# One encoder layer on one core: query and key tiles split during the output projections, selection steps set apart, gate tiles loaded in four pieces, gathers spread to near the end

## The chip, the cores and the metric

One core of a Trainium2 chip runs the whole layer as one program. The metric is the device time of one execution in microseconds (us), compared as a median of several runs. Engines: PE (TensorE, matrix products), ACT (ScalarE), DVE (VectorE), POOL (GpSimd, here mainly an issuer of transfers) and SP (SyncE, the issuer of all other transfers). Each engine works its own instructions strictly in the order in which the program emits them.

## The reference, cut to what matters

```python
n = rmsnorm(h, g_mix);  proj = n @ w_in            # h: 16 meta tokens + 512 tokens, D = 1024
y_hy = hyena_branch(...);  y_rg = rglru_branch(...)
merged = sigmoid(gA) * y_hy + sigmoid(gB) * y_rg
h = h + merged @ w_out
h = h + peer(rmsnorm(h, g_ffn), wq, keys, u_tab, v_tab);  out = rmsnorm(h, g_final)[16:]

def peer(x, ...):                                   # 8 heads, 128 keys a half, top 16, 16384 experts
    q = (x @ wq).reshape(B, L, 8, 2, 128)
    s = einsum('blhpd,hpkd->blhpk', q, keys);  ts, ti = top_k(s, 16)
    cand = ts[..., 0, :, None] + ts[..., 1, None, :];  cs, ci = top_k(cand, 16)
    experts = e1 * 128 + e2;  g = softmax(cs)       # e1, e2: ti taken at ci // 16, ci % 16
    act = gelu(x . u_tab[experts]) * g
    return sum over experts of act * v_tab[experts]
```

## The kernel before, in words

Every product is made exact to about float32 by splitting each operand into a float16 high and a low part (`split`, L80: ACT writes the high part, L81; DVE the low part, L82) and running three float16 matmuls (`mm3`, L84). Weights come as a list of jobs, [128, 1024] float32 tiles of 512 KB. `w_load` (L94) issues a job's load on SP into one of three buffers `wf` (six once the pool `gp` exists), `w_prep` (L103) splits it into one of four buffers `wh`, and `w_get(i)` (L120) first prepares up to job i + 2. So the split of a weight is emitted two jobs ahead of its matmuls.

The order of the work: the **front** (Hyena and RG-LRU branches); the **output projections**, eight pairs of jobs hy_out and rg_out merged into `mg`, then eight jobs w_out, a sum of squares and the second norm; the **Q stage**, 16 query projections with 16 weights wq and 2 key tiles (jobs w0 to w0 + 17), scores, and the first top-16 selections; then the **expert stage**. It computes, for 384 of the 512 tokens, all 128 blocks of experts densely: step u_e is gelu(x . u) of block e (24 matmuls of 384 columns), step v_e adds block e's weighted values (18 matmuls of 512 columns). The job list `seq` runs u_0 to u_100, then v_96, u_101 ... alternating until u_127, then v_0 to v_95. The results of u_0 to u_95 are spilled to DRAM (`sd`) and loaded again (`sin`). The last 128 tokens (tile tt = 3) take gathered rows instead: 128 gathers of u rows and 128 of v rows (`gather`, L1093, an indirect transfer of 128 rows of 4 KB from POOL's queue, four row buffers), each followed by one DVE instruction (L1128, L1149).

Beside u_0 to about u_93 the program places **selection and routing**: 64 top-16 selections (`top16`), then `routing`: `select(tt)` for each token tile (eight candidate top-16s, index arithmetic, a softmax whose tanh runs on ACT, transposes on PE, expansion copies on ACT) and `tokens(tt)`, which in 16 blocks of 8 tokens builds one-hot products `oh` and `og` on DVE. `flush` multiplies those of two blocks earlier on PE into `ps_gt` (three buffers), and ACT moves them to `stg`, from where they go to DRAM as the gate table `gd`. `both` interleaves tokens(0) with select(1), and tokens(1) with select(2).

How much of it stands beside one step is set by hand. Each `yield` of these generators names its cost on DVE and ACT in microseconds, and `pull` (L800) takes from the generators until a step's budget is used up; what was overdrawn is carried on. A `yield 0` ends the step. The budgets are 3.2 in a query step and `PACE` = 3.7 in a u step, where each gather step taken is also charged 1.3. `gathers(rate)` allows `rate` gather steps per step: `GRATE` = 0.7 beside routing, 1.35 after it, and from v_0 on (268 - steps done) / (E0 - 12). When routing has ended, or at u_93 at the latest, the remaining routing is forced out, the pools change, and the first gate tile `gin` (16 experts, 3 MB) is loaded: eight experts at once and eight one step later. Later gate tiles are loaded whole, at the fifth step of every 16 (`gload`, `pmul`).

Of the kernel before, what the change touches and what calls it, by code (L numbers as in the profile page):

```python
# [66 lines left out]
class Kernel:  # L67
    def __init__(self, ctx, tc, a, out):
        self.ctx, self.tc, self.nc, self.a, self.out = ctx, tc, tc.nc, a, out
        self.keep = ctx.enter_context(tc.tile_pool(name="keep", bufs=1))  # L70
        self.wp = ctx.enter_context(tc.tile_pool(name="wp", bufs=1))
        self.jobs = []
        self.loaded = {}
        self.ready = {}
        self.nl = 0
        self.evac = None
        self.nr = 0
        self.gp = None

    def split(self, hi, lo, src, s):  # L80
# [13 lines left out]
    def w_load(self, upto):  # L94
        while self.nl <= min(upto, len(self.jobs) - 1):
            src, s, n, dst = self.jobs[self.nl]
            p = self.wp if self.gp is None or self.nl % 2 else self.gp
            t = p.tile([128, D], F32, name="wf", bufs=self.WF)
            self.nc.sync.dma_start(t[:, :n], src)  # L99
            self.loaded[self.nl] = t  # L100
            self.nl += 1

    def w_prep(self, upto):  # L103
        while self.nr <= min(upto, len(self.jobs) - 1):
            i = self.nr
            self.w_load(i)
            src, s, n, dst = self.jobs[i]
            t = self.loaded.pop(i)
            if dst is None:
                h = self.wp.tile([128, 2, D], F16, name="wh", bufs=self.WH)  # L110
                hi, lo = h[:, 0, :n], h[:, 1, :n]
                self.ready[i] = h
            else:
                hi, lo = dst()
                self.ready[i] = None
            self.split(hi, lo, t[:, :n], s)
            self.nr += 1
            self.w_load(i + self.WF * (1 if self.gp is None else 2))
# [165 lines left out]
    def front(self, xt, acc):  # L284
# [220 lines left out]

        mp = ctx.enter_context(tc.tile_pool(name="mp", bufs=1, side="right"))
        mg = fr.tile([128, 2, 8, SEQ], F16, name="mg", tag="n")
        for i in range(8):
# [15 lines left out]
            nc.vector.scalar_tensor_tensor(ma, ma, (S_W * S_YR) / (S_HO * S_YH), mb, op0=OP.mult, op1=OP.add)  # L524
            self.split(mg[:, 0, i, :], mg[:, 1, i, :], ma, 0.5 * S_M / (S_W * S_YR))
        sq, qs = {}, None
        for i in range(8):
# [12 lines left out]
            if i == 0:  # L540
                qs = sq.pop(0)
        pn = psum.tile([128, 2, 512], F32, name="ps_n2", tag="pg")
        for k, t in enumerate((qs, sq[6], sq[7])):
# [271 lines left out]
    def peer(self, acc):  # L815
# [40 lines left out]
        def half_topk(h, t):  # L856
            for pr in range(2):
                for tt in (3, 0, 1, 2):
                    hp = 2 * h + pr
                    self.top16(qp, t[:, pr, tt, :], tv[:, tt, hp, :], ti[:, tt, hp, :], 128)  # L860
                    yield 1.3

# [3 lines left out]
        for i in range(16):  # L866
            if i == 0:
                ws = [self.w_get(w0 + k) for k in range(2)]
                pj = {k: psum.tile([128, 512], F32, name="ps_q", tag="s", bufs=3) for k in range(2)}
# [12 lines left out]
            if i == 3:  # L882
                self.w_prep(w0 + 6)
            if i % 2 == 1 and i >= 3:
# [4 lines left out]
            if i >= 3:  # L889
                self.pull(3.2, 3.2)  # L890

# [19 lines left out]

        def gload(k, parts=((0, EB),)):
            if k < 128 // EB:
                b = order[EB * k] // EB
                if b not in gin:
                    gin[b] = vp.tile([128, NCH, EB, CH], F32, name="gin", bufs=2)
                for i, n in parts:
                    o = CH * (EB * b + i)
                    nc.sync.dma_start(gin[b][:, :, i:i + n, :].rearrange("p c e t -> p c (e t)"),
                                      gd[:, :, o:o + CH * n].rearrange("c p n -> p c n"))  # L920

# [6 lines left out]
        def pmul(i):  # L928
            if i >= 128:
                return  # L930
            e = order[i]
            if i % EB == 4:
                gload(i // EB + 1)
            sload(i + 6)
# [56 lines left out]
        for pos, (kind, e) in enumerate(seq):  # L991
            if kind == "u":
# [14 lines left out]
                if vp is None and (route not in self.bgq or e == E0 - 3):  # L1007
# [10 lines left out]
                    ob += [ups.tile([128, 2, 512], F32, name="ob%d" % k, tag="ob%d" % k) for k in range(3)]  # L1018
                    gload(0, ((0, 8),))
                    e0 = e  # L1020
                elif vp is not None and e == e0 + 1:
                    gload(0, ((8, EB - 8),))
                    nc.vector.tensor_scalar(self.ident, self.ident, S_P * S_V, None, op0=OP.mult)
                continue
# [9 lines left out]
            if i >= 128 - E0:  # L1034
                if rate is None:
                    rate = (268 - self.gsteps) / (E0 - 12.0)
                gathers(rate)
            else:
                gathers(self.GRATE[1])
# [41 lines left out]
    LV = 5  # L1081
    PACE = (3.7, 3.7)
    TB = 8
    GRATE = (0.7, 1.35)
    LAG = 2
# [13 lines left out]
    def gather_setup(self, psum, e12, w):  # L1099
# [9 lines left out]
        nc.vector.tensor_tensor(xg, x2[:, 0, :, TD:], x2[:, 1, :, TD:], OP.add)  # L1109
        yield 2.0  # L1110
        for b in range(2):
            pt = psum.tile([128, 512], F32, name="ps_xn", tag="t", bufs=2)
# [63 lines left out]
    def routing(self, p, psum, tv, ti, iota, iof, gd):  # L1176
        nc = self.nc
        eT = {}

        def select(tt):  # L1180
            t4 = p.tile([128, 256, 4], F16, name="t4")
# [53 lines left out]
            sh = [128, 8, TOPK]  # L1235
            nc.vector.tensor_tensor(t, cv, cv[:, :, 0:1].to_broadcast(sh), OP.subtract)
            nc.scalar.activation(t, t, AF.Tanh, scale=-0.5)
            yield 0.3
            yield 0
            nc.vector.tensor_scalar(w, t, -1.0, 1.0, op0=OP.mult, op1=OP.add)  # L1240
# [6 lines left out]
            yield 2.4  # L1247
            yield 0
            if tt == 3:
# [4 lines left out]
            nc.tensor.transpose(pt[:, 128:256], e12[:, 0, :], self.ident)  # L1254
            nc.tensor.transpose(pt[:, 256:384], w.rearrange("p h k -> p (h k)"), self.ident)

            ed = p.tile([128, 128, 2, 4], F16, name="ed", bufs=2)
# [4 lines left out]
            wt = pt[:, 256:384, None].to_broadcast([128, 128, 4])  # L1262
            nc.scalar.activation(gd4[:, :, 0, :], wt, AF.Copy, scale=S_G)
            nc.vector.scalar_tensor_tensor(gd4[:, :, 1, :], wt, S_G, gd4[:, :, 0, :], op0=OP.mult, op1=OP.subtract)
            eT[tt] = ed, gd4
            yield 1.0, 2.0

# [194 lines left out]
```

## Time and profile before

| | us |
|---|---|
| runs shown (three) | 1713.04, 1717.74, 1720.14; median 1717.74 |
| the profiled execution | 1716.81 (span from first to last instruction 1715.0) |
| PE busy | 1619.6 (94% of the span) |
| DVE busy | 1402.8 (82%) |
| ACT busy | 767.4 (45%) |
| POOL busy | 368.9 (22%) |
| mean granted clock of PE | 0.982 of full |

The span is what the trace covers; the 1.8 us outside it belong to launch and end. Busy time of DVE counts the overlap of consecutive instructions once in the page's totals; in sums by mean duration the overlap is counted twice, so the prediction uses distances from start to start where it can. In tables by stage the columns are busy time (and count) of each engine, PE's granted clock (1.00 is 2.4 GHz, 0.50 is 1.2 GHz), the busy share of the 16 DMA engines and what they moved.

### The profile page before, as it was taken

Reading aid. Unit: us, or ns where it says so; the run is one execution under the profiler, and the core shown is the slowest. Engines: PE = TensorE matmul, PEld = TensorE weight load, DVE = VectorE, ACT = ScalarE, POOL = GpSimd, SP = SyncE. Lnnn points to the kernel's source line nnn. Section 1 sums busy time; section 2 is a strip of 40 time slices with the busy share of each in tenths; the row PEclk is TensorE's granted clock in tenths of the full one; section 3 lists DMA queues with packets and bytes.
Section 4 is the critical chain, followed back from the end, with each engine's and each line's share of the span. In section 5 each row is a group of like instructions: output and inputs, shape, how many; then the busy total and the mean of one; then the engine's idle time right before and its main releaser. Section 6 shows DMA issues by size and latency. Waiting matters only on the chain. (4 is left out here: it accounts for less than half of the span.)

```text
span 1715.0 us, 25010 instructions
## 1 busy us (share of the span) xinstructions
PE 1619.6 (94%) x9451; PEld 905.7 (53%) x9451; DVE 1402.8 (82%) x2422; ACT 767.4 (45%) x1055; POOL 368.9 (22%) x321
## 2 busy tenths in 40 slices
PE   7999999899989987998998998899999999999998
PEld 5675666444435544665665665455554444444443
DVE  7736679985478998998997996788889889999984
ACT  5433379962243333443754764343333333324342
POOL 0000000000000001222221223344445444445500
PEclk9999999999999999999998999999999999999999
DMA  5332142223323347678887899999999999999981
GB/s 194 124 121 74 40 146 65 71 80 106 113 86 96 89 146 249 236 239 306 280 312 263 299 343 348 350 383 314 366 359 361 406 395 393 400 395 407 395 307 50
DMA packets 134970, 416.19 MB, mean 243 GB/s; under 512 B 12064, under 2 KB 39968, under 8 KB 131392
## 3 DMA queue, kind: packets, MB, share of 16 engines
q1 hardware_dynamic: 97776, 279.72, 46.0%
q0 software_dynamic: 37072, 134.86, 21.0%
q8 instruction: 74, 1.21, 0.3%
q14 instruction: 48, 0.39, 0.1%
HBM read 368.39 MB, written 46.14 MB: 242 GB/s over the span
## 5 line engine op out<-in xcount | busy, mean ns | idle before, releaser
L981 PE MATMUL ob<-wh,pt 128*128 128x512 f16 x2304 | 511.9, 380 | 19.2 <-DVE wh L82 11.8
L82 DVE SCALAR_TENSOR_TENSOR wh<-wf,wh 128x1024 f16<-128x1024 f32 (+1 forms) x340 | 409.2, 1207 | 103.5 <-ACT wh L81 102.5
L81 ACT ACTIVATE wh<-wf 128x1024 f16<-128x1024 f32 (+1 forms) x340 | 352.5, 1041 | 142.1 <-DMA wf<-in_peer_v 48.3
L981 PEld LDWEIGHTS <-pt 128*128 128x128 f16 x2304 | 225.9, 98 | 288.6 <-issue 23.0
L88 PE MATMUL ps_e<-x,wh 128*128 128x384 f16 x1024 | 337.1, 329 | 16.2 <-DVE wh L82 16.2
L86 PE MATMUL ps_e<-x,wh 128*128 128x384 f16 x1024 | 337.6, 330 | 1.9 <-ACT gs L955 1.9
L87 PE MATMUL ps_e<-x,wh 128*128 128x384 f16 x1024 | 337.5, 330 | 0.0
L1095 POOL DMA_INDIRECT rows<-in_peer_un,gidx x128 | 182.1, 1423 | 446.8 <-DVE junk L1128 394.0
L88 PEld LDWEIGHTS <-wh 128*128 128x128 f16 x1504 | 148.3, 99 | 149.1 <-DVE wh L82 23.6
L1095 POOL DMA_INDIRECT rows<-in_peer_v,gidx x128 | 180.1, 1407 | 187.3 <-DVE acc L1149 154.9
L87 PEld LDWEIGHTS <-wh 128*128 128x128 f16 x1504 | 148.3, 99 | 129.5 <-issue 12.1
L86 PEld LDWEIGHTS <-wh 128*128 128x128 f16 x1504 | 148.6, 99 | 120.9 <-issue 4.7
L1149 DVE SCALAR_TENSOR_TENSOR acc<-rows,dots,acc 128x1024 f32<-128x1024 f32 x127 | 162.9, 1282 | 20.6 <-DMA rows<-in_peer_v,gidx 19.8
L943 ACT ACTIVATE pt<-pf 128x384 f16<-128x384 f32 x128 | 66.6, 520 | 226.2 <-DVE pf L936 167.5
L1128 DVE SCALAR_TENSOR_TENSOR junk<-rows,xn 128x1024 f32<-128x1024 f32 x128 | 156.2, 1220 | 5.6 <-DMA rows<-in_peer_un,gidx 5.0
L271 PE MATMUL ps_p<-n,wh 128*128 128x264 f16 x960 | 111.9, 277 | 2.0 <-DVE wh L82 2.0
L955 ACT ACTIVATE gs<-ps_e 128x384 f32<-128x384 f32 x96 | 47.2, 491 | 132.3 <-PE ps_e L88 121.0
L271 PEld LDWEIGHTS <-wh 128*128 128x128 f16 x960 | 94.2, 98 | 20.5 <-issue 3.5
L1290 ACT ACTIVATE stg<-ps_gt 128x512 f32<-128x512 f32 x96 | 93.1, 1083 | 15.8 <-PE ps_gt L1283 10.5
L947 DVE TENSOR_TENSOR pt<-pf,pt 128x384 f16<-128x384 f32 x128 | 70.9, 554 | 12.4 <-ACT pt L943 12.4
L86 PE MATMUL ps_p<-n,wh 128*128 128x512 f16 x192 | 73.3, 382 | 0.1
L87 PE MATMUL ps_p<-n,wh 128*128 128x512 f16 x192 | 73.3, 382 | 0.0
(276 smaller groups left out, 1832.7 us busy)
## 6 DMA issues: line engine op xcount, KB each, us to landing
wf<-in_peer_u SPq DMA_DIRECT2D x128, 512.0 KB
wf<-in_peer_v SPq DMA_DIRECT2D x128, 512.0 KB
gd<-stg SPq DMA_DIRECT2D x24, 1024.0 KB
wf<-in_w_in SPq DMA_DIRECT2D x44, 512.0 KB
gin<-gd SPq DMA_DIRECT2D x7, 3072.0 KB
sd<-gs SPq DMA_DIRECT2D x48, 384.0 KB
sin<-sd SPq DMA_DIRECT2D x48, 384.0 KB
wf<-in_wq SPq DMA_DIRECT2D x16, 512.0 KB
```

Source lines behind the costliest of these rows:

```text
L81: self.nc.scalar.activation(hi, src, AF.Copy, scale=s)
L82: self.nc.vector.scalar_tensor_tensor(lo, src, s, hi, op0=OP.mult, op1=OP.subtract)
L86: mm(ps, lh, rh, start=first, stop=False)
L87: mm(ps, lh, rl, start=False, stop=False)
L88: mm(ps, ll, rh, start=False, stop=last)
L271: nc.tensor.matmul(ps[:, h, :HL], x, n[:, y, c, h * HL:(h + 1) * HL], start=(c == 0 and x is lh and y == 0), stop=(c == 7 and x is ll))
L947: nc.vector.tensor_tensor(pt[i][:, 1, :], pf.pop(i), pt[i][:, 0, :], OP.subtract)
L981: mm(ob[tt][:, h, :], pp[:, x, sl], w[:, y, h * 512:(h + 1) * 512], start=first and k == 0, stop=last and k == 2)
L1095: self.nc.gpsimd.indirect_dma_start(out=r, out_offset=None, in_=table, in_offset=bass.IndirectOffsetOnAxis(ap=self.gidx[:, j:j + 1], axis=0))
L1128: nc.vector.scalar_tensor_tensor(junk, rows.pop(0), 1.0, self.xn, op0=OP.mult, op1=OP.mult, accum_out=self.dots[:, j:j + 1])
L1149: nc.vector.scalar_tensor_tensor(acc2, r, d, acc2, op0=OP.mult, op1=OP.add)
L1290: nc.scalar.activation(st[c][:, :, o:o + 4].rearrange("p e t -> p t e"), ps, AF.Copy, scale=S_P / S_G)
```

## The change

1. While the output projections run, 18 jobs (16 wq, 2 key tiles) are loaded through POOL's queue, split, and written back to DRAM as float16 pairs (`pre`), 1.75 per pair of projections and then 1.5 per w_out job. In the Q stage SP loads these pairs straight into `wf` or `wh` buffers, and the keys into their tile, with no split.
2. Pacing: a key top-16 is charged 1.65 instead of 1.3; the query budget is 4.4 and 4.2 instead of 3.2, `PACE` 4.2, `GRATE` 0.8 and 1.5.
3. In `select` and `gather_setup`, steps that hand over between engines are set apart by further yields. For tiles 0 and 3 each is a `yield 0`; for tiles 1 and 2, which run interleaved with `tokens`, one or two yields of 0.001.
4. The gate tile is loaded in four pieces of six token chunks each: the first one at four successive steps from the end of routing, later ones at steps 3, 5, 7 and 9 of 16.
5. The final gather rate spreads the rest over E0 - 5 steps instead of E0 - 12.

```diff
+    NPRE = 18
+    PS = (1.75, 1.5)
+    def pre_load(self):
+        while self.npl < min(self.np + 4, self.NPRE):
+            t = self.pool_p.tile([128, D], F32, name="pw", bufs=5)
+            self.nc.gpsimd.dma_start(t, self.jobs[self.w0 + self.npl][0])
...
+    def presplit(self, k, load=True):
+        self.pcr += k
+        while self.pcr >= 1.0:
+            self.pcr -= 1.0
...
+            h = self.pool_p.tile([128, 2, D], F16, name="ph", bufs=5)
+            self.split(h[:, 0, :], h[:, 1, :], self.pl.pop(self.np), self.jobs[self.w0 + self.np][1])
+            self.nc.gpsimd.dma_start(self.pre[self.np], h)
+            self.np += 1
+            if load:
+                self.pre_load()
@@ w_load
+            if self.is_pre(self.nl):
...
+                    nm, nb = ("wf", self.WF) if k % 2 else ("wh", self.WH)
+                    t = self.wp.tile([128, 2, D], F16, name=nm + "p", tag=nm, bufs=nb)
+                    self.nc.sync.dma_start(t, self.pre[k])
@@ front
+        self.pool_p = mp
+        self.pre_load()
...
+            self.presplit(self.PS[0])
...
+            self.presplit(self.PS[1] if i < 7 else 0)
...
@@ peer
-                    yield 1.3
+                    yield 1.65
-                self.pull(3.2, 3.2)
+                self.pull(4.4, 4.2)
-        def gload(k, parts=((0, EB),)):
+        def gload(k, q):
...
+                cs = slice(q * NCH // 4, (q + 1) * NCH // 4)
+                nc.sync.dma_start(gin[b][:, cs].rearrange("p c e t -> p c (e t)"),
+                                  gd[cs, :, CH * EB * b:CH * EB * (b + 1)].rearrange("c p n -> p c n"))
-            if i % EB == 4:
-                gload(i // EB + 1)
+            if i % EB in (3, 5, 7, 9):
+                gload(i // EB + 1, (i % EB - 3) // 2)
-                    rate = (268 - self.gsteps) / (E0 - 12.0)
+                    rate = (268 - self.gsteps) / (E0 - 5.0)
-    PACE = (3.7, 3.7)
+    PACE = (4.2, 4.2)
-    GRATE = (0.7, 1.35)
+    GRATE = (0.8, 1.5)
@@ routing, select
+        def gap(tt, n):
+            if tt in (0, 3):
+                yield 0
+            else:
+                for _ in range(n):
+                    yield 1e-3
             nc.vector.tensor_tensor(t, cv, cv[:, :, 0:1].to_broadcast(sh), OP.subtract)
+            yield 0.3
+            yield from gap(tt, 2)
             nc.scalar.activation(t, t, AF.Tanh, scale=-0.5)
-            yield 0.3
-            yield 0
+            yield 0.0, 0.3
+            yield from gap(tt, 2)
...
             nc.tensor.transpose(pt[:, 256:384], w.rearrange("p h k -> p (h k)"), self.ident)
+            yield from gap(tt, 1)
...
             nc.scalar.activation(gd4[:, :, 0, :], wt, AF.Copy, scale=S_G)
+            yield 0.0, 2.0
+            yield from gap(tt, 2)
             nc.vector.scalar_tensor_tensor(gd4[:, :, 1, :], wt, S_G, gd4[:, :, 0, :], op0=OP.mult, op1=OP.subtract)
```

## Rows read from the trace of the kernel before

**Rows 1.** The page's first part: the span, and PE's busy time with its number of instructions.

```profile
span 1715.0 us, 25010 instructions
PE 1619.6 (94%) x9451; PEld 905.7 (53%) x9451; DVE 1402.8 (82%) x2422; ACT 767.4 (45%) x1055; POOL 368.9 (22%) x321
```

**Rows 2.** Busy time by stage: the front; the output projections; the Q stage; u_0 to u_22; u_23 to u_92; u_93 to the first matmuls of v_96; the alternation of u and v; v_0 to v_79. Columns: stretch, its length, busy time and count of PE, PEld, DVE, ACT and POOL, granted clock, DMA share, GB/s.

```profile
0.00:374.40 374.40, 354.48 (x2197) 228.10 (x2198) 278.83 (x402) 221.69 (x316) 6.11 (x64) 0.98 0.30 101
374.40:479.30 104.90, 99.43 (x453) 44.77 (x453) 59.62 (x76) 32.31 (x44) 0.00 (x0) 0.99 0.34 108
479.30:575.70 96.40, 94.47 (x553) 47.27 (x553) 80.24 (x287) 37.33 (x53) 0.00 (x0) 0.98 0.29 93
575.70:691.60 115.90, 96.37 (x587) 56.16 (x584) 106.25 (x427) 40.03 (x57) 5.49 (x5) 0.97 0.56 180
691.60:1028.40 336.80, 320.71 (x2395) 207.75 (x2393) 305.31 (x497) 183.85 (x242) 79.88 (x48) 0.97 0.80 284
1028.40:1088.80 60.40, 48.46 (x303) 28.17 (x301) 36.07 (x51) 24.67 (x33) 17.71 (x13) 0.89 0.97 344
1088.80:1310.60 221.80, 221.80 (x1183) 115.64 (x1182) 188.76 (x268) 83.07 (x115) 98.55 (x77) 1.00 0.97 355
1310.60:1643.50 332.90, 319.78 (x1490) 147.93 (x1489) 305.18 (x351) 117.41 (x158) 161.16 (x114) 1.00 1.03 398
```

**Rows 3.** What PE waited for, over the whole span: who, for whom, us in total, times, longest.

```profile
PE ps_gt L1283 <- ACT stg L1290: 18.4, 12, 5.8
PE ps_e L88 <- DVE wh L82: 16.2, 13, 2.2
PE ob L981 <- DVE wh L82: 11.8, 16, 1.5
...
PE ob L981 <- ACT pt L943: 6.1, 1, 6.1
...
PE ps_xn L1114 <- DVE xg L1109: 4.6, 1, 4.6
...
PE ps_q L88 <- DVE wh L82: 1.7, 1, 1.7
```

**Rows 4.** The same table as in rows 2 for short stretches: u_5 and u_6; u_21 to u_29; u_45 and u_46; u_70 and u_71; u_93 and u_94; u_101 and v_96.

```profile
596.20:607.10 10.90, 8.14 (x50) 4.53 (x48) 10.49 (x51) 2.91 (x5) 0.00 (x0) 1.00 0.49 132
683.80:718.90 35.10, 35.10 (x218) 21.16 (x217) 32.24 (x90) 14.41 (x21) 6.95 (x4) 1.00 0.68 243
782.20:800.00 17.80, 10.80 (x67) 6.39 (x65) 16.77 (x25) 4.81 (x7) 4.28 (x3) 0.81 0.84 304
906.50:921.80 15.30, 11.48 (x66) 6.80 (x64) 13.28 (x21) 4.76 (x7) 5.02 (x3) 0.78 0.69 251
1028.40:1048.70 20.30, 14.48 (x116) 9.37 (x114) 12.90 (x16) 11.25 (x13) 5.15 (x3) 0.83 0.98 373
1072.10:1088.80 16.70, 10.58 (x45) 4.71 (x43) 8.76 (x15) 5.68 (x9) 2.81 (x2) 0.80 0.85 338
```

**Rows 5.** DVE in order of time (start, duration, instruction): a key top-16 from its first MAX8 to the next one's, and one stretch with the one-hot products, a gather's product and the low part of a weight.

```profile
505.46 0.29 DVE L1170 MAX8 tv<-sc 128x8 f32<-128x128 f32 x1
...
506.91 0.28 DVE L1170 MAX8 tv<-sc 128x8 f32<-128x128 f32 x1
...
1028.62 1.23 DVE L1305 TENSOR_TENSOR oh<-iota,ed 128x2048 f16<-128x2048 f16 x1
1029.76 1.22 DVE L1128 SCALAR_TENSOR_TENSOR junk<-rows,xn 128x1024 f32<-128x1024 f32 x1
...
1030.90 1.22 DVE L82 SCALAR_TENSOR_TENSOR wh<-wf,wh 128x1024 f16<-128x1024 f32 x1
1032.04 1.22 DVE L1309 TENSOR_TENSOR og<-oh,gd 128x2048 f16<-128x2048 f16 x1
```

**Rows 6.** What DVE waited for in the output projections, 374.4 to 479.3 (columns as in rows 3).

```profile
DVE ma L522 <- PE ps_hy L88: 14.7, 7, 2.4
...
DVE xt L536 <- PE ps_o L88: 8.5, 8, 1.6
```

**Rows 7.** What ACT waited for in selection, routing and the start of the values, 575.7 to 1088.8 (columns as in rows 3).

```profile
ACT wh L81 <- DMA wf<-in_peer_u: 34.7, 8, 8.8
ACT sm_t L1237 <- DVE sm_t L1236: 29.6, 4, 9.8
ACT ed L1260 <- PE ps_r L1255: 11.2, 3, 3.7
```

**Rows 8.** The page's part on transfers: tiles, issuing queue, count, size of one.

```profile
wf<-in_peer_u SPq DMA_DIRECT2D x128, 512.0 KB
...
gin<-gd SPq DMA_DIRECT2D x7, 3072.0 KB
...
sin<-sd SPq DMA_DIRECT2D x48, 384.0 KB
```

**Rows 9.** POOL's gather instructions from u_23 to u_92 (busy time, mean ns of one, idle time before them and for whom).

```profile
L1095 POOL DMA_INDIRECT rows<-in_peer_un,gidx x48 | 79.9, 1664 | 266.7 <-DVE junk L1128 266.7
```

**Rows 10.** The same in the alternation of u and v.

```profile
L1095 POOL DMA_INDIRECT rows<-in_peer_un,gidx x63 | 79.6, 1263 | 101.1 <-DVE junk L1128 94.0 <-issue 5.2 <-DVE wh L82 0.9
```

**Rows 11.** The chain that ended last, two pieces of it (start, us, what).

```profile
1056.99 20.66 DMA wf<-in_peer_u
...
1350.72 9.38 DMA rows<-in_peer_v,gidx
```

More of the change, by code (lines that the diff above doesn't have):

```diff
@@ L78, in __init__, with pre_drain, is_pre @@
         self.gp = None
+        self.dr0 = ctx.enter_context(tc.tile_pool(name="dr0", bufs=1, space=DRAM))
+        self.pre = self.dr0.tile([self.NPRE, 128, 2, D], F16, name="pre")
+        self.pool_p = None
+        self.np = self.npl = 0
+        self.pcr = 0.0
+        self.pl = {}
+        self.w0 = None
+    NPRE = 18
[4 more added lines that the diff above has]
+            self.nc.gpsimd.dma_start(t, self.jobs[self.w0 + self.npl][0])
+            self.pl[self.npl] = t
+            self.npl += 1
+    def presplit(self, k, load=True):
+        self.pcr += k
+        while self.pcr >= 1.0:
+            self.pcr -= 1.0
+            if self.np >= self.NPRE or (not load and self.np >= self.npl):
+                return
+            h = self.pool_p.tile([128, 2, D], F16, name="ph", bufs=5)
[4 more added lines that the diff above has]
+                self.pre_load()
+    def pre_drain(self):
+        self.pcr = 0.0
+        self.presplit(self.npl - self.np, False)
+    def is_pre(self, i):
+        return self.w0 is not None and self.w0 <= i < self.w0 + self.NPRE
     def split(self, hi, lo, src, s):
@@ L96, in w_load @@
             src, s, n, dst = self.jobs[self.nl]
+            if self.is_pre(self.nl):
+                k = self.nl - self.w0
+                assert k < self.np
+                if dst is None:
+                    nm, nb = ("wf", self.WF) if k % 2 else ("wh", self.WH)
+                    t = self.wp.tile([128, 2, D], F16, name=nm + "p", tag=nm, bufs=nb)
+                    self.nc.sync.dma_start(t, self.pre[k])
+                    self.loaded[self.nl] = t
+                else:
+                    self.loaded[self.nl] = dst
+                self.nl += 1
+                continue
             p = self.wp if self.gp is None or self.nl % 2 else self.gp
@@ L108, in w_prep @@
             t = self.loaded.pop(i)
+            if self.is_pre(i):
+                self.ready[i] = None
+                if dst is None:
+                    self.ready[i] = t
+                else:
+                    for r, x in enumerate(dst()):
+                        self.nc.sync.dma_start(x, self.pre[i - self.w0, :, r, :])
+                self.nr += 1
+                self.w_load(i + self.WF)
+                continue
             if dst is None:
@@ L541, in front @@
                 qs = sq.pop(0)
+            self.presplit(self.PS[1] if i < 7 else 0)
+        self.pre_drain()
+        assert self.np == self.NPRE, self.np
         pn = psum.tile([128, 2, 512], F32, name="ps_n2", tag="pg")
@@ L868, in peer @@
                 ws = [self.w_get(w0 + k) for k in range(2)]
+                self.w_prep(w0 + 6)
                 pj = {k: psum.tile([128, 512], F32, name="ps_q", tag="s", bufs=3) for k in range(2)}
@@ L881, in peer @@
                              x2[:, 0, c, :], x2[:, 1, c, :], c == 0, c == 7)
-            if i == 3:
-                self.w_prep(w0 + 6)
             if i % 2 == 1 and i >= 3:
@@ L916, in gload @@
                     gin[b] = vp.tile([128, NCH, EB, CH], F32, name="gin", bufs=2)
[L917 to L920, printed above, removed]
+                cs = slice(q * NCH // 4, (q + 1) * NCH // 4)
+                nc.sync.dma_start(gin[b][:, cs].rearrange("p c e t -> p c (e t)"),
+                                  gd[cs, :, CH * EB * b:CH * EB * (b + 1)].rearrange("c p n -> p c n"))
         def sload(i):
@@ L1018, in peer @@
                     ob += [ups.tile([128, 2, 512], F32, name="ob%d" % k, tag="ob%d" % k) for k in range(3)]
-                    gload(0, ((0, 8),))
+                    gload(0, 0)
                     e0 = e
-                elif vp is not None and e == e0 + 1:
-                    gload(0, ((8, EB - 8),))
-                    nc.vector.tensor_scalar(self.ident, self.ident, S_P * S_V, None, op0=OP.mult)
+                elif vp is not None and e in (e0 + 1, e0 + 2, e0 + 3):
+                    gload(0, e - e0)
+                    if e == e0 + 1:
+                        nc.vector.tensor_scalar(self.ident, self.ident, S_P * S_V, None, op0=OP.mult)
                 continue
@@ L1178, in routing @@
         eT = {}
+        def gap(tt, n):
+            if tt in (0, 3):
+                yield 0
+            else:
+                for _ in range(n):
+                    yield 1e-3
         def select(tt):
@@ L1247, in select @@
             yield 2.4
-            yield 0
+            yield from gap(tt, 2)
             if tt == 3:
@@ L1263, in select @@
             nc.scalar.activation(gd4[:, :, 0, :], wt, AF.Copy, scale=S_G)
+            yield 0.0, 2.0
+            yield from gap(tt, 2)
             nc.vector.scalar_tensor_tensor(gd4[:, :, 1, :], wt, S_G, gd4[:, :, 0, :], op0=OP.mult, op1=OP.subtract)
             eT[tt] = ed, gd4
-            yield 1.0, 2.0
+            yield 0.7
         pend = []
```

## The prediction, made before the changed kernel was run

> **What bounds the kernel now.** The first view is the busy time of the engines: PE is busy for 94% of 1715.0 us [rows 1], so a gain can only come from the 95 us in which PE stands, and from stretches in which its clock is down. The second view is busy time by stage [rows 2]. A stage's loss is its length less PE's busy time, plus (1 - granted clock) times its length. That gives 23.0 us for u_0 to u_22 (19.5 idle and 3.5 by the clock), 26.2 for u_23 to u_92 (16.1 and 10.1), 18.5 from u_93 to v_96 (11.9 and 6.6), nothing in the alternation of u and v, and 13.1 from v_0 to v_79. The front loses more, but the change does not touch it.
>
> The third view, PE's waits, tells why [rows 3]: 16.2 us for low parts of weights from DVE beside the u steps, 18.4 for a free `ps_gt`, which ACT empties, 4.6 for `xg` before the transposes, 6.1 before v_96, 11.8 for low parts in the v steps. The fourth view is steps [rows 4]. Nine undisturbed u steps take 35.1 us, 3.90 each; with that, the alternation (26 u and 31 v steps in 221.8 us, rows 2) gives 3.88 for a v step. u_5 and u_6 take 10.9 us, 5.45 each. The cause is on DVE: a key top-16 takes 1.45 us from start to start and a weight's low part 1.14 [rows 5], and three selections and one low part are 5.49. DVE sets the pace there, and PE waits.
>
> The waits for `ps_gt` have another cause. ACT waited 29.6 us in four places for the difference that the softmax's tanh reads, and 11.2 in three for the transposes [rows 7]. Behind these in ACT's order stand the copies that free `ps_gt`. At two such places PE lost 7.0 and 3.8 us idle, with a mean clock of 0.81 and 0.78 [rows 4].
>
> **The change part by part.** All sums are made against the profiled execution, 1716.8 us, 1.8 outside its span; the median of the runs is 0.9 above it.
>
> *Splits moved to the output projections.* 18 low parts of 1.14 us, 20.5 us of DVE, and as many high parts on ACT leave the Q stage for a stage in which DVE is busy for 59.6 of 104.9 us and ACT for 32.3 [rows 2]. A pair of projections lasts (24 + 12) products, 7.8 us by the same rate as the v step's (3.88 for 18). DVE stands about 2.1 us of it before the sums, 14.7 over 7 [rows 6], and 1.75 splits are 2.0 us. It fits. Transfers are 18 loads, 18 stores and 18 loads again instead of 18 loads, 19 MB more; the DMA share is 0.34 there. What could show is the first load, issued when the branch buffers come free, as ACT stands before the first split until it has landed; two jobs of lead cover most. I take a cost of 1.5 us, bounds 0 and, by rival D, much more.
>
> One row speaks against the place of issue. POOL's gathers take 1664 ns beside the one-hot products and 1263 later [rows 9, 10], so its issuing does depend on what DVE does. The Trainium skill, page SBUF — State Buffer, section SBUF: two separate sides, says that a transfer issued by GpSimd has its descriptors written by that engine, which an exclusive lock of DVE's on their shared port can hold up. Here it would be 0.4 us on each of 36 issues, which nobody waits for with four loads ahead.
>
> *What the Q stage does with it.* It gets 4.4 for selections charged 1.65, by the rule of `pull` 35 selections before u_0, where it had 33. Most of the DVE time that comes free idles. The wait of 1.7 us [rows 3] goes.
>
> *u_0 to u_22.* 4.2 / 1.65 is 2.55 selections a step: 2.55 x 1.45 + 1.14 = 4.83, still 0.93 above 3.90. Some ten steps wait so, less the 1.3 us of score products at u_8: 8.0. The index work of tiles 3 and 0 behind them is charged about 1.12 times its length (1.25 against 1.14 for a one-hot product), so 4.2 is 3.75, with the low part 4.89, 0.99 too much over four full steps: 4.0. Together 12. The wait for `xg` goes, as a step now lies between it and the transposes, and with it the fall of the clock, which came in that wait. 23.0 becomes 12: gain 11; bounds 0 (the DVE waits grow by what the others give) and 15.
>
> *u_23 to the end of routing.* I counted what `pull` takes by the yields. Routing ends beside u_89 (before: u_93, by force). From u_23 to u_88 DVE has 317 us by the distances of rows 5 and the lines of the selection, and PE 298 (66 steps of 3.90, 90 groups of four gate products at 0.45, an estimate from busy 320.7 less 10.1 less 70 steps in rows 2). DVE is 19 us longer; it starts some 6 ahead, so 13 are waits. Before, DVE had 310 and PE 313, and the loss was ACT's. Now the tanh comes two token steps after the difference (2 x 1.14 us of DVE work or more), the copies two after the transposes; ACT is busy only 184 of 337 us and catches up. I leave 3 us of these waits. 26.2 becomes 16: gain 10; bounds 0 and 20.
>
> *The end of routing.* Eight copies and six product groups remain in one step, before it was ten and eight, with DVE now up to 5 us behind PE. The loss was 9.3, 5.8 idle and 3.5 by the clock [rows 4]; I take 9: gain 0.5, bounds -4 and 4.
>
> *The first v step.* 9.4 us are lost at u_101 and v_96 [rows 4]: a load of `wf` took 20.66 us [rows 11] behind 3 MB of gate tile [rows 8], asked for nine steps before v_96. The tile is now asked for in four pieces from u_89 on, 13 steps ahead. The same bytes pass in a busy stage (0.97), so I keep 2: gain 7.5, bounds 0 and 9.4.
>
> *The alternation.* 1.5 gathers a step instead of 1.35: two weights, three rows of 0.52 MB each and 0.2 MB of gate tile in 7.78 us, 362 GB/s. The next stage moves 398 [rows 2], so it holds; a cost of 1, bounds 0 and 6.
>
> *The values.* By the counts 139 gather steps are done at v_0 before, 158 after. The rate falls from (268 - 139) / 84 = 1.54 to (268 - 158) / 91 = 1.21. A v step moves a weight (0.52 MB), the gathers, 0.2 of `gin` and 0.2 of `sin`: 1.72 MB before, which at 398 GB/s [rows 2] is 4.3 us; now 1.55, 3.90 against PE's 3.88. DVE, busy 305 of 332.9 us, loses 0.33 x 1.2 = 0.4 us a step. So the waits of 13.1 us nearly go; smaller pieces also spare `sin` and `wf` the queue behind 3 MB. Left: 2 us, gain 11; bounds 4 and 13. The last gather now ends beside about v_88, and its closing sums fit before v_95.
>
> Sum: 1.7 + 11 + 10 + 0.5 + 7.5 + 11 - 1.5 - 1 = 39.2. 1716.8 - 39 = 1678 us, clock included.
>
> **The rivals.**
>
> B, DVE stays the bound: what ACT's waits gave up, DVE's lag takes, since `PACE` asks 4.89 us of DVE against 3.90 of PE wherever no gate products stand. For it: 33 selections become only 35, and DVE exceeds PE by 19 us in routing. Against: DVE stood idle in ACT's waits before. Without the 11 and 10: 1716.8 - 18 = 1699.
>
> C, transfers bind the expert stage. The trace moves 398 GB/s over 332.9 us [rows 2] and 344 with a share of 0.97 around v_96. If the gathers at 1.5 with the pieces of the gate tile let u_90 to v_96 lag, the gain of 7.5 goes, and a V stage at 380 GB/s (4.08 a step) waits 0.2 x 88 = 18 us. Then 1678 + 7.5 + 18 = 1704. The sum above needs none of the next sentences. The Trainium skill, page DMA: Bandwidth & Descriptors, section Specifications, gives about 358 GB/s as what HBM gives one core. By that a v step took 4.33, and the time would be 1678 + 7.5 + 0.45 x 88 = 1725. The trace's 398 speaks against it.
>
> D, on the other side: the splits' loads are late. ACT stands before each of the 18 until its tile has landed, the high parts of the projections' weights stand behind it, and PE stops. 18 splits lie in eight pairs and three steps, 8 x 7.8 + 3 x 5.2 = 78 us, 4.3 us each. POOL's queue has to pass a load and a store in that time, and a store waits for its split. One transfer takes 8 to 9 us from issue to landing by the chain [rows 11]. With four loads ahead it holds. If only one load were under way at a time, a period were 8 us, 66 us more: 1678 + 66 = 1744. The change turns into a loss from 4.3 + 39 / 18 = 6.5 us a period on.
>
> **How the numbers follow.** Chances: forecast 0.65, B 0.19, C 0.10, D 0.06. A measurement of this kernel can tell 0.5%, 8.6 us, from no change. The bounds of no change are 1708 and 1725. The forecast, B and most of C lie below; of B I put 0.03 and of C 0.02 into no change, and of C 0.02 beside D into slower. Faster 0.87, same 0.05, slower 0.08. With every term halfway to its better bound the sum is 51 (1666), halfway to its worse one 17 (1700); the forecast's own range, 1662 to 1695, lies about there. The range of 8 in 10 takes in B and most of C and, below, routing's upper bound: 1658 to 1707.
>
> **What would show it.** Right: no wait for `ps_gt` over 3 us before routing's end, none for `xg`; no fall of the clock between u_19 and u_88; waits for low parts beside u_5 to u_80 of 20 to 28 us in total; v_96 within 3 us of u_101's end; v_0 to v_79 in about 320 us; no wait over 1 us in the output projections. Wrong: waits of ACT for `pw` (rival D), long waits of PE for low parts in routing above 30 us (B), or a V stage that keeps 4.1 us a step (C).

## The result, and the profile after

The changed kernel took 1677.2 us (median; 1676.4 to 1679.1) where the kernel before took 1715.4 beside it on the same chip: ratio 0.9775, 95% interval 0.9751 to 0.9798. Forecast were 1678, with a range of 1658 to 1707. The profiled execution took 1676.4, 1.8 outside its span.

The page's first part, to hold against [rows 1]:

```profile
span 1674.6 us, 25103 instructions
PE 1611.2 (96%) x9451; PEld 901.4 (54%) x9451; DVE 1405.8 (84%) x2422; ACT 768.1 (46%) x1055; POOL 362.9 (22%) x357
```

DVE and ACT do what they did before, to 3 us; POOL has 36 instructions more, the transfers of the early splits. So no engine was given less work: the 40 us are waits and clock.

Busy time by stage, with the columns of [rows 2]: the front; the output projections; the Q stage; u_0 to u_22; u_23 to u_88; u_89 to the first matmuls of v_96; the alternation; v_0 to v_79.

```profile
0.00:375.30 375.30, 355.80 (x2197) 229.01 (x2198) 278.86 (x401) 221.58 (x316) 6.14 (x64) 0.98 0.30 100
375.30:483.30 108.00, 100.41 (x454) 44.38 (x454) 76.84 (x93) 48.13 (x60) 19.09 (x36) 0.99 0.82 299
483.30:578.30 95.00, 94.86 (x553) 47.50 (x553) 64.60 (x291) 22.11 (x37) 0.00 (x0) 0.97 0.21 68
578.30:683.40 105.10, 94.10 (x588) 55.05 (x586) 98.43 (x375) 39.35 (x56) 6.22 (x5) 1.00 0.61 188
683.40:996.60 313.20, 303.53 (x2316) 196.07 (x2314) 309.39 (x531) 181.23 (x238) 85.33 (x51) 0.99 0.87 305
996.60:1059.10 62.50, 56.15 (x364) 33.83 (x362) 41.34 (x57) 24.73 (x33) 24.49 (x20) 0.97 1.03 401
1059.10:1287.00 227.90, 226.18 (x1200) 117.37 (x1201) 203.62 (x275) 87.61 (x121) 99.45 (x88) 1.00 1.00 374
1287.00:1603.10 316.10, 316.10 (x1489) 148.13 (x1488) 292.60 (x339) 117.73 (x160) 122.14 (x96) 1.00 1.03 395
```

Three lines matter. The projections became longer (104.9 to 108.0). The Q stage has DVE busy for 65 of 95 us: the room that the early splits made is not used. And v_0 to v_79 has PE busy for its whole length, 316.1 for 332.9. The sixth and seventh lines can't be set beside those of [rows 2] as they stand: there the cut (1088.8) lies at the end of v_96, here at its start. From the start of v_96 to v_0 the alternation took 228.3 before and 227.9 after.

What PE waited for, over the whole span, against [rows 3]:

```profile
PE ps_e L126 <- DVE wh L120: 16.3, 16, 1.7
...
PE ps_gt L1362 <- ACT stg L1369: 3.8, 11, 0.8
PE ps_e L124 <- ACT gs L1019: 2.3, 1, 2.3
PE ob L1045 <- ACT pt L1007: 2.1, 1, 2.1
PE ob L1045 <- DVE wh L120: 1.7, 2, 1.4
PE ps_hy L126 <- DVE wh L120: 1.6, 2, 0.9
```

`ps_gt` fell from 18.4 to 3.8, the low parts of the v steps from 11.8 to 1.7, `xg` is gone; the low parts of the u steps stayed (16.2 and 16.3): a step still asks more time of DVE than of PE. ACT, in selection and routing, with [rows 7] to compare:

```profile
ACT sm_t L1313 <- DVE sm_t L1310: 13.3, 4, 5.5
...
ACT ed L1337 <- PE ps_r L1331: 3.5, 2, 2.8
```

29.6 became 13.3, with the longest at 5.5 instead of 9.8; the wait for the transposes fell from 11.2 to 3.5.

### The profile page after: what moved, and what is told of

Same layout as the page of the kernel before. It is cut to its first block, busy times and chain, and to the rows that moved or that the text cites. A ratio compares the mean times of both kernels' runs of the same rounds, so it can differ in the third digit from the quotient of the medians.

```text
span 1674.6 us, 25103 instructions
## 1 busy us (share of the span) xinstructions
PE 1611.2 (96%) x9451; PEld 901.4 (54%) x9451; DVE 1405.8 (84%) x2422; ACT 768.1 (46%) x1055; POOL 362.9 (22%) x357
## 3 DMA queue, kind: packets, MB, share of 16 engines
q0 software_dynamic: 42256, 153.73, 24.4%
## 4 chain that ended last, share of the span: by engine, by line
PE 55%; issue 18%; DVE 12%; POOL 6%; DMA 5%; ACT 4%; POOLq 0%; DVEq 0%; SPq 0%; ACTq 0%
PE ob L1045 29%; POOL rows L1160 6%; PE ps_p L331 4%; DVE wh L120 2%; PE ps_e L126 2%; PE ps_e L124 2%; PE ps_e L125 2%; DMA rows<-in_peer_un,gidx 2%; PE ps_q L125 2%; PE ps_q L126 1%; PE ps_q L124 1%; DMA wf<-in_peer_u 1%; PE ps_p L124 1%; PE ps_p L125 1%; PE ps_p L126 1%
## 5 line engine op out<-in xcount | busy, mean ns | idle before, releaser
L1045 PE MATMUL ob<-wh,pt 128*128 128x512 f16 x2304 | 506.4, 379 | 3.9 <-ACT pt L1007 2.1
L120 DVE SCALAR_TENSOR_TENSOR wh<-wf,wh 128x1024 f16<-128x1024 f32 (+1 forms) x324 | 388.0, 1207 | 74.2 <-ACT wh L119 73.9
L119 ACT ACTIVATE wh<-wf 128x1024 f16<-128x1024 f32 (+1 forms) x324 | 335.9, 1039 | 94.3 <-DMA wf<-in_peer_u 37.6
L126 PE MATMUL ps_e<-x,wh 128*128 128x384 f16 x1024 | 335.5, 328 | 16.3 <-DVE wh L120 16.3
L126 PEld LDWEIGHTS <-wh 128*128 128x128 f16 x1376 | 135.0, 98 | 137.2 <-DVE wh L120 29.6
L1160 POOL DMA_INDIRECT rows<-in_peer_v,gidx x128 | 156.5, 1223 | 239.6 <-DVE acc L1215 219.9
L125 PEld LDWEIGHTS <-wh 128*128 128x128 f16 x1376 | 135.2, 98 | 109.9 <-issue 6.3
L124 PEld LDWEIGHTS <-wh 128*128 128x128 f16 x1376 | 135.1, 98 | 103.9 <-issue 1.7
L331 PEld LDWEIGHTS <-wh 128*128 128x128 f16 x960 | 94.4, 98 | 20.4 <-issue 3.5
L1011 DVE TENSOR_TENSOR pt<-pf,pt 128x384 f16<-128x384 f32 x128 | 71.4, 558 | 12.7 <-ACT pt L1007 11.8
## 6 DMA issues: line engine op xcount, KB each, us to landing
sin<-sd SPq DMA_DIRECT2D x48, 384.0 KB, 13.1
```

The costliest lines, as they stand in the source:

```text
L119: self.nc.scalar.activation(hi, src, AF.Copy, scale=s)
L120: self.nc.vector.scalar_tensor_tensor(lo, src, s, hi, op0=OP.mult, op1=OP.subtract)
L124: mm(ps, lh, rh, start=first, stop=False)
L125: mm(ps, lh, rl, start=False, stop=False)
L126: mm(ps, ll, rh, start=False, stop=last)
L331: nc.tensor.matmul(ps[:, h, :HL], x, n[:, y, c, h * HL:(h + 1) * HL], start=(c == 0 and x is lh and y == 0), stop=(c == 7 and x is ll))
```

## The experiments

Each kernel was timed against the kernel before on its own chip, so they are compared by ratio; an interval is some 0.2 to 0.3% either way, 3 to 5 us. Where less counts, the traces are compared step by step.

**Part 3 undone** (selection steps together again).

```diff
-            yield 0.3
-            yield from gap(tt, 2)
             nc.scalar.activation(t, t, AF.Tanh, scale=-0.5)
-            yield 0.0, 0.3
-            yield from gap(tt, 2)
+            yield 0.3
+            yield 0
...
```

> The changed kernel with part 3 undone: the selection steps stand together again, as in the kernel before; all else as changed. Theory (the routing stage gained because ACT no longer stands before a difference or a transpose with the copies that free ps_gt behind it): the waits of PE for ps_gt and xg and the falls of the clock come back. Before they were 18.4 and 4.6 us and the clock cost 10.1 us in u_23 to u_92; with the budgets of the changed kernel I expect 20 to 35 us more than the changed kernel's 1677, so about 1702, with 15 us or more of waits for ps_gt and at least four new falls of the clock. Rival (the DVE time freed and the new budgets ended the waits): within 5 us of 1677, and waits for ps_gt under 6 us.

Measured: 1710.9, ratio 0.9956 (0.9939 to 0.9972), some 31 us above the changed kernel's. Two groups of PE's waits, and one of ACT's, came back:

```profile
PE ps_gt L1356 <- ACT stg L1363: 24.4, 12, 8.5
...
PE ps_xn L1179 <- DVE xg L1174: 4.6, 1, 4.6
```

```profile
ACT sm_t L1310 <- DVE sm_t L1309: 38.9, 4, 11.8
```

and the granted clock (0.96) in u_23 to u_84:

```profile
689.40:1007.80 318.40, 292.00 (x2204) 188.81 (x2203) 295.90 (x485) 171.83 (x226) 80.55 (x49) 0.96 0.81 280
```

All of it came back, and more than there had been before (24.4 us of waits for `ps_gt` against 18.4). That the larger budgets let DVE fall further behind at such a place would explain the rest; no run tests it. By the steps of the two traces, 32.5 us apart in span, 6.4 lie in u_0 to u_22 and 22.5 in routing. The other 4 come after routing: 9.8 us are lost beside u_93 and u_94 (one wait of 7.5 for `gs`), where the changed kernel loses 5.8 from u_99 on; that these belong to the order is not shown. The theory holds, for some 29 us.

**Part 3 alone**, on the kernel before (the same lines, added).

> The kernel before with part 3 alone: the selection steps set apart, nothing else changed. Theory (part 3 carries the gain of selection and routing by itself): the 18.4 us of waits for ps_gt fall below 8, the 4.6 for xg go, and most of the falls of the clock; DVE's own lag takes some of it back, and more of routing is forced at u_93. The running sum gives 24 us less; 1717 less 24 is 1693, taken between 1688 and 1700; the value stage keeps its 13 us of waits. Rival (it needs the room that the other parts make): 10 us or less, 1707 or more.

Measured: 1695.0, ratio 0.9871 (0.9842 to 0.9900), 22 us less. PE's waits for `ps_gt` fell from 18.4:

```profile
PE ps_gt L1296 <- ACT stg L1303: 7.8, 8, 2.2
```

The value stage keeps its loss and adds to it (v_0 to v_79 in 337 us for 333). One part makes more than half of the whole gain, alone as well as last.

**Part 1 undone** (`NPRE` = 0; job w0 + 6 prepared at the fourth query step again, as before).

> The changed kernel with part 1 undone: the 18 query and key tiles are split in the Q stage again, with its larger budget of 4.4; all else as changed. Theory (the freed DVE time of the Q stage mostly idles, and PACE alone sets the waits of u_0 to u_22): the output projections come back by about 3 us (108.0 to 105), the Q stage loses 2 to 5 (DVE then has some 85 of 95 us of work there, waits for low parts return), u_0 to u_22 lose 0 to 3 as DVE starts them later; in sum 1677 with 4 either way. Rival (the freed time is what u_0 to u_22 gained 10.8 us from): about 1688, with 10 us or more lost there.

Measured: 1673.7, ratio 0.9744 (0.9728 to 0.9761): the changed kernel is not slower without its early splits but faster, by 5 us by ratio, where the intervals just overlap, and by 3.4 by its trace. The output projections:

```profile
376.20:481.10 104.90, 99.43 (x453) 44.74 (x453) 59.62 (x76) 32.32 (x44) 0.00 (x0) 0.99 0.33 108
```

are as before, the Q stage takes 96.8 for 95.0, and u_0 to u_22 take 105.0, in the changed kernel 105.1. So no part of the gain of u_0 to u_22 came from freed DVE time. These stages make 1.3 of the 3.4 us (3.1 less 1.8); 2.2 lie in the alternation, which here has no wait.

**Part 2 undone** (1.3, 3.2 and `PACE` 3.7; gather rates kept).

> The changed kernel with the budgets of before: 1.3 for a selection, 3.2 in a query step, PACE 3.7; the gather rates 0.8 and 1.5 stay. 33 selections before u_0; 3.7 / 1.3 is 2.85 selections a step, 4.13 us and 1.14 for the low part, 5.27 of DVE; routing is not done at u_93 and its rest is forced there. Theory: u_0 to u_22 give back 6 of the 10.8 us they gained (xg stays cured), and the forced end costs 4 to 10 more; 1687 to 1693, taken 1688. Rival (the budgets don't matter beside the steps set apart): 1677 to 1680.

Measured: 1680.4, ratio 0.9785 (0.9768 to 0.9803): the rival's figure was right, 2 us by ratio, less than the noise. But not because budgets don't matter. By the steps of the trace, u_0 to u_22 lose 3.9 us more. From u_23 to u_84 it takes 277 us for 294: 24 groups of gate products fewer stand there (10.7 us at the 0.445 a group used below), and 6.7 us less is lost. The rest of routing is forced into u_93, which alone takes 27.4, with 22 groups in it; 8.2 us more are lost from there to u_98. Gains and losses cancel but for the 3.0 us between the spans.

**A larger query budget alone.**

```diff
-                self.pull(4.4, 4.2)
+                self.pull(5.8, 5.8)
```

> The changed kernel with a larger query budget: 5.8 in place of 4.4, so 46 selections stand before u_0 where it has 35; PACE stays 4.2. DVE idles some 30 of the 95 us of the Q stage in the changed kernel, and 11 selections of 1.45 us are 16. Theory (the u steps wait because PACE asks 4.89 us of DVE in a step in which PE has 3.90, and that is so as long as selection and routing last): the waits stay and only routing ends earlier, by five steps; no gain, 1674 to 1679. Rival (the waits are the sum of the DVE work that is left): 9 to 11 us faster, 1667.

Measured: 1678.8, ratio 0.9776 (0.9758 to 0.9793), no gain. Routing ended at u_84, five steps earlier, and there the kernel stood at 975.3 us; the changed one, less five steps of 3.90, at 977.1. The waits for low parts stayed (16.3 before, 14.5 here), as the theory said; what was won went later, in the longer of the two waits for `gs`, beside u_91:

```profile
PE ps_e L126 <- DVE wh L120: 14.5, 16, 1.6
PE ps_e L124 <- ACT gs L1019: 11.0, 2, 8.7
```

**The larger query budget with a smaller `PACE`** (6.2 and 3.8).

> The changed kernel with a query budget of 6.2 (49 selections before u_0) and PACE 3.8 in place of 4.2. Theory: with 3.8, 3.8 / 1.65 is 2.3 selections a step, 3.3 us, and 1.14 for the low part, 4.5 of DVE; routing lasts to u_93 as its work starts seven steps earlier. A running sum of the three engines in the order of the program, from the durations of the rows, gives 9.6 us of waits of PE up to u_101 where it gives 24.9 for the changed kernel (measured there some 25), so 15 us less, 1662; some 3 may go at the start, as DVE has 80 us of work in the 77 from the first selection to u_0. Rival (waits for low parts come late because their loads or ACT are late, not by DVE's pace): no change, 1677.

Measured: 1665.3, ratio 0.9697 (0.9679 to 0.9714), 13 us less. From u_23 to u_84 it takes 278 us for 294; ten groups of gate products fewer stand there (4.5 us), the other 11.5 are loss that is gone. The waits of PE:

```profile
PE ps_e L126 <- DVE wh L120: 9.4, 7, 2.5
...
PE ob L1045 <- ACT pt L1007: 6.0, 1, 6.0
```

The first is nearly halved. The second, at v_96, is back: routing now ends eight steps ahead of it instead of twelve. It takes the gathers too, for with fewer of them and the same end of routing it is gone (both edits, below). A smaller `PACE` alone was not run, so how the 13 us divide between the two edits is not shown.

**Part 4 undone** (gate tiles whole, the first in two halves).

> The changed kernel with part 4 undone: the first gate tile in two halves, later ones whole; all else as changed. Theory (the pieces help the first v step only): u_99 to v_96 lose 9 to 10 us in place of about 5.7, and 0 to 3 us of waits come at the later gate tiles; 1679 to 1684, taken 1681. Rival (3 MB transfers in front of weights and spilled values made the waits of the value stage): 11 us or more of waits come back from v_0 to v_79, 1690 or more.

Measured: 1679.9, ratio 0.9774 (0.9758 to 0.9791), the same as changed. The trace shows 3.8 us more from u_85 to v_96, with a wait of 3.6 before u_98, and v_0 to v_79 to 0.1 us as in the changed kernel: the pieces do nothing for the value stage.

**The old gather rates.**

```diff
-                    rate = (268 - self.gsteps) / (E0 - 5.0)
+                    rate = (268 - self.gsteps) / (E0 - 12.0)
-    GRATE = (0.8, 1.5)
+    GRATE = (0.7, 1.35)
```

> The changed kernel with the gather rates of before: 0.7 and 1.35 a step, the rest spread over E0 - 12 steps; all else as changed. By the count of yields 141 gather steps are then done at v_0 and the rate is 1.51 a v step, where the changed kernel has 158 and 1.21. Theory (the value stage was held up by its gather rate): 9 to 13 us of waits for low parts come back from v_0 to v_79, the alternation and the first v step give back 0 to 2; about 1687. Rival (the smaller pieces of the gate tile cured the value stage): at most 3 us, so 1677 to 1680.

Measured: 1690.8, ratio 0.9834 (0.9817 to 0.9850), 10 us above the changed kernel by ratio, 16 by the spans, all of it from v_20 to v_79. Is it DVE or the bytes? The old rates ask more of both, so DVE's part was halved: the sum takes half of the columns of each gathered row, the same rows are moved, and the values of the other half are left out.

```diff
-                nc.vector.scalar_tensor_tensor(acc2, r, d, acc2, op0=OP.mult, op1=OP.add)
+                nc.vector.scalar_tensor_tensor(acc2[:, :512], r[:, :512], d, acc2[:, :512],
+                                               op0=OP.mult, op1=OP.add)
```

> The kernel with the old gather rates once more, with each sum of a gathered v row taken over only half of its columns: DVE's instruction is half as long, and the transfers are the same (the values of the last 128 tokens are left out in the other half). From v_0 to v_79 the run with the old rates took 328.4 us, the changed kernel 312.2. Theory (the old rate asks 1.72 MB in a step of 3.93 us, 437 GB/s, where both move some 400: bytes bind): the waits stay, v_0 to v_79 take 322 to 329, DMA moves about 400 GB/s, and the time stays near 1690. Rival (DVE binds: its 1.2 us for each row, 1.5 times a step): with half of them gone, 0.9 us a step, the waits vanish, 312 to 316, and the time falls to some 1677.

Measured: 1690.5, ratio 0.9841 (0.9822 to 0.9861). The stretch from 1370 to 1600, first in the changed kernel, then with the old rates:

```profile
1370.00:1600.00 230.00, 230.00 (x1090) 108.87 (x1088) 211.17 (x244) 84.73 (x117) 85.08 (x70) 1.00 1.03 394
1370.00:1600.00 230.00, 221.98 (x1041) 103.88 (x1040) 213.58 (x246) 79.68 (x107) 102.42 (x82) 1.00 1.04 400
```

and then with the old rates and half of the sums, and what ACT waited for in it:

```profile
1370.00:1600.00 230.00, 221.89 (x1037) 104.07 (x1036) 167.53 (x238) 79.22 (x106) 98.21 (x79) 0.99 1.04 399
```

```profile
ACT wh L119 <- DMA wf<-in_peer_v: 118.2, 45, 7.0
```

With 46 us less of DVE work PE is busy for the same 222 of 230. DVE now waits for ACT, and ACT for weights. The bytes bind, at 400 GB/s. (The Trainium skill, page Perfetto Trace Analysis, section Roofline, says that one core alone may draw more than its share of 358 GB/s, up to about 435 by its DMA engines. The runs here agree that 358 is no limit, and over such a stretch they stop at 400 of the 435.)

**Fewer gathers before v_96**, more after it.

```diff
-                    gathers(self.GRATE[1])
+                    gathers(self.GRATE[1] if vi else self.GRATE[0])
-    GRATE = (0.8, 1.5)
+    GRATE = (0.8, 1.65)
```

> The changed kernel with 0.8 gather steps a step (not 1.5) from the end of routing until v_96, and 1.65 (not 1.5) in the alternation. Theory (the 3 MB of the first gate tile come on top of a stage in which the gathers take all the bandwidth that is left; the wait is for bytes): some eight gathers, 4 MB, leave that stage; of the 15.9 us at u_89 and u_90 nothing goes, the losses from u_99 to v_98, some 5 us, go; 1672. Rival (the wait is for SP's queue, which stands at a store of the gate table): no change.

Measured: 1670.3, ratio 0.9729 (0.9712 to 0.9746), by the spans 6.3 us less. From u_91 to u_101, first the changed kernel (46.7 us, to v_96), then this one:

```profile
1012.40:1059.10 46.70, 43.41 (x267) 25.74 (x265) 31.45 (x45) 15.48 (x22) 21.33 (x17) 1.00 1.04 399
```

```profile
1012.10:1055.00 42.90, 42.90 (x266) 25.81 (x265) 24.10 (x34) 15.87 (x24) 8.50 (x9) 1.00 1.03 391
```

The first runs at the 400 GB/s of the value stage; with half of the gathers left out PE does not wait, neither here nor in the alternation (198.5 us from v_96 to u_127 for 200.7). The rival, that SP's queue stands at a store of the gate table, would have kept the wait.

**Both edits that helped** (6.2, 3.8, and the rates of the last one).

> The changed kernel with both edits that helped: the query budget of 6.2 with PACE 3.8, and 0.8 gather steps a step until v_96, then 1.65. If the waits for DVE in selection and the waits for bytes before v_96 are separate, the gains add: 15 and 6 to 7 off the changed kernel, about 1657. If the shorter way from routing's end (u_93) to v_96 leaves too few steps for the 3 MB gate tile even so, a wait of 3 to 6 us stays there: 1661.

Measured: 1657.3, ratio 0.9654 (0.9625 to 0.9682). The gains add.

**Further**: `PACE` 3.75, gathers at 0.6 beside routing, 0.8 until v_96, then 1.75, and

```diff
-    PS = (1.75, 1.5)
+    PS = (1.4, 1.0)
```

> As the combined one, and further: PACE 3.75, gathers 0.6 beside routing, 0.8 until v_96, 1.75 in the alternation, and the splits beside the output projections spread evenly (1.4 a pair, then 1.0). Theory: routing ends beside u_89, so there are twelve steps for the gate tile; the running sum gives 2 us less of waits and one fall of the clock less (4 to 6 us); the projections give back 1 to 2 of the 3 us that the splits cost there; about 1651. Against it: 154 gather steps at v_0 leave 1.25 a v step, 0.916 + 0.524 x 1.25 = 1.57 MB in 3.93 us, 400 GB/s, which is what the old rates moved in the value stage (400) while they waited; if that is the limit, 2 to 5 us of waits come back there.

Measured: 1652.2, ratio 0.9625 (0.9596 to 0.9654), 25 us faster than the changed kernel. The output projections, and v_0 to v_79:

```profile
374.60:480.10 105.50, 99.44 (x454) 44.80 (x454) 77.09 (x93) 47.84 (x60) 19.09 (x36) 0.98 0.84 306
1259.90:1576.00 316.10, 316.10 (x1490) 148.13 (x1489) 292.61 (x340) 117.95 (x159) 141.06 (x104) 1.00 1.04 399
```

The same 18 splits and transfers (DMA share 0.84) now cost the projections 0.6 us instead of 3.1. The value stage stands at its 399 GB/s and PE does not wait: it is at the edge, not over it, with 104 gathers in 80 steps, 1.30 a step (the 1.25 of the expectation was a miscount).

## Why the prediction was right, and where it was not

The sum was 39.2 and came out at 40.4 by the spans. So close a hit is partly luck: the terms that came out better than forecast make 10.1 us together, those that came out worse, with the front, 8.9. To measure them alike, each stretch is set against its work at the undisturbed pace: 3.90 us a u step, 0.445 a group of gate products (u steps with two groups and no wait take 4.79), 1.3 for the score products in u_0 to u_22, 11.7 from u_99 to v_96 and 198.5 from there to u_127 (the run with fewer gathers), 316.1 for v_0 to v_79.

| step of the prediction | gain forecast | lost before | lost after | gain measured |
|---|---|---|---|---|
| projections | -1.5 | | | -3.1 |
| Q stage | 1.7 | | | 1.4 |
| u_0 to u_22 | 11 | 24.9 | 14.1 | 10.8 |
| u_23 to routing's last step | 10 | 24.6 | 15.7 | 8.9 |
| end of routing, to u_98 | 0.5 | 9.0 | 5.6 | 3.4 |
| first v step | 7.5 | 6.3 | 3.6 | 2.7 |
| alternation | -1 | 2.6 | 2.2 | 0.4 |
| values | 11 | 16.8 | 0 | 16.8 |

The remaining -0.9 is the front, which the change does not touch.

**Right.** The two causes in selection and routing, kept apart: ACT's order (part 3; 31 us undone, 22 alone) and DVE's pace against PE's. In u_0 to u_22 "23.0 becomes 12" came out as 24.9 and 14.1, each some 2 higher, so that the gain was met; 6.4 of its 10.8 us come back with part 3 undone and 3.9 with the old budgets. "4.2 is 3.75, with the low part 4.89" against 3.90 foretold that the waits for low parts would stay; they are 16.3 us, and 16 us more of selections before u_0 hardly moved them (14.5) until `PACE` fell too (9.4). "Most of the DVE time that comes free idles": with the early splits undone u_0 to u_22 took the same. By what would show it: no wait for a free `ps_gt` over 0.8 (one of 1.2 at it was for `og` from DVE), none for `xg`, v_96 2.1 us after u_101's end, no wait over 0.9 in the products of the projections, v_0 to v_79 in 316.1 us. The low parts came to 16.3, under the 20 to 28 named, and, against the forecast of none, one fall of the clock was left between u_19 and u_88, beside u_73 after two waits of 1.2 and 0.8 us.

**The values, mis-sized.** "The waits of 13.1 us nearly go ... Left: 2 us". Lost before were 16.8, not 13.1, and nothing is left. The step that failed is the floor: I took PE's busy time, 319.8 in [rows 2], for its work, and the same steps undisturbed take 316.1. The cause was named right, 1.72 MB a step before and 1.55 after against some 400 GB/s. The run with half of the sums shows that it was bytes and not DVE's "0.4 us a step".

**The first v step, mis-sized in the other direction.** 9.4 were counted there; by the steps they are 6.3 up to the start of v_96 and 2.6 after it. And "asked for in four pieces from u_89 on, 13 steps ahead ... I keep 2" left out of the sum that the gathers were raised from 1.35 to 1.5 in the same stage; only rival C had it. The stage was full (401 GB/s from u_89 to v_96), and 5.8 were lost from u_99 through the alternation, where I had kept 2 and 1. The pieces are worth 3.8 by the trace, at most; leaving out half of the gathers is worth all of the 5.8.

**The splits in the projections.** "DVE stands about 2.1 us of it ... and 1.75 splits are 2.0 us. It fits." 1.75 a pair is two in three pairs of four, 2.28 us, and that does not fit: PE waited for low parts of `wh`. At 1.4, two in two pairs of five, it does: no wait for `wh` is left there. So the cost was neither transfers nor POOL's place of issue, both of which are the same in the last run. Rival D asked for waits of ACT for `pw`; there was one of 0.8.

```profile
POOL pre L106 <- DVE ph L120: 61.4, 12, 7.7
...
ACT ph L119 <- DMA pw<-in_wq: 0.8, 1, 0.8
```

This is from the projections of the changed kernel: POOL stood before 12 of the 18 stores for the split, with the next load behind it, but four loads ahead were enough.

**The end of routing.** Forecast as nearly unchanged; it gave 3.4, with one wait of 2.3 for `gs` in place of 5.8 us idle.

**The rivals.** B was half true: DVE still holds PE up from u_0 to u_88. Some 30 us are lost there after the change (15.7, and 14.1 in u_0 to u_22 beside 89.7 of steps and 1.3 of scores), 16.3 of them as waits for low parts; but ACT's waits had come on top. C was half true as well: it put the loss at u_90 to v_96, with the gathers at 1.5, and there the transfers did bind, so that 2.7 of the 7.5 us came. For the value stage, its larger part, it was wrong: 395 GB/s, and no wait. But the limit is near. 400 GB/s in 316.1 / 80 = 3.95 us is 1.58 MB; 0.916 of it are the weight, the gate tile and the spilled values, a gather is 0.524, which leaves 1.27 gathers a step. By the gathers issued from v_0 to v_79 the changed kernel has 1.20 a step (96), the kernel before 1.43 (114, less than the 1.54 that its rate asks), and the fastest run held 1.30 (104) without a wait.

**Open.** u_0 to u_22 still lose some 11 us in the fastest run (102.4 less 89.7 and 1.3). Why the wait for the full stage fell on one spot of 7.5 to 8.7 us in four runs (on `gs`, whose store had not landed) and in three of 1.2, 2.1 and 1.4 in the changed kernel was not settled; with fewer gathers it was not there.

## What to carry to other kernels

Where a slow hand-over between two engines stands in the order of a third's work, put other work between its two halves before tuning budgets: this was worth 22 us alone and 31 undone last, while a larger query budget alone, or the old budgets again, moved it by 2 or less by ratio. A budget that asks more of an engine in a step than the step lasts makes waits however early the work begins; moving work and lowering the rate together gave 13 us where moving work alone gave nothing. Count the bytes that a step asks for at PE's pace against what the trace moves when it is full, and spread optional transfers so that each stage stays below it.

## What was not expected of the hardware

PE's busy time holds stalls: v_0 to v_79 show 319.8 us busy while PE waited, and 316.1 without a wait, for the same products. A short wait can cost nearly its length again in clock. After 1.2 and 0.8 us of waits close together the granted clock in the changed kernel was down to its lower level of 1.2 GHz for the next stretch, 1.7 us of loss:

```profile
918.60:922.00 3.40, 3.40 (x13) 1.64 (x11) 3.40 (x5) 3.40 (x6) 1.68 (x1) 0.51 0.47 189
```

(0.51 is the granted clock.) Eight waits of 1.0 to 1.7 us spread over u_5 to u_18 brought no fall (clock 1.00 in that stage). And over long stretches the transfers reach the same 399 to 401 GB/s in three different mixes: gate tile with gathers, weights with gathers at 1.30 a step, and weights with the gathers of the old rates, which ask 1.51.
